# One encoder layer on one core: a third of the feed-forward block products in a seven-product form, weight sums on VectorE, the feed-forward axis in four chunks

## The chip, the core and the metric

The kernel runs on one core of a Trainium2 chip. The time is device microseconds (us) of one execution; the figure for the kernel before is the median of three runs. In the text PE is the matmul engine (TensorE), PEld its weight loads, DVE is VectorE, ACT is ScalarE, POOL is GpSimd, SP is SyncE, which issues most DMAs. PSUM is the memory in which matmuls accumulate: eight banks of 128 x 512 float32.

## What is computed

One layer over 256 tokens with 2048 features (D) and a feed-forward width (d_ff) of 5632. The two feed-forward networks (FFNs), one ahead of the mixers and one behind, are

```python
def swiglu(h, w1, w3, w2):
    return (jax.nn.silu(h @ w1) * (h @ w3)) @ w2

x = x + 0.5 * swiglu(rmsnorm(x, g1), w1, w3, w2)     # FFN 1
h = rmsnorm(x, g)
# h @ w_in, differential attention y_a, latent attention y_b
x = x + (sigmoid(g_a) * (y_a @ W_a) + sigmoid(g_b) * (y_b @ W_b)) @ W_out
x = x + 0.5 * swiglu(rmsnorm(x, g2), w1', w3', w2')  # FFN 2
```

Everything is float32. w1 and w3 are 2048 x 5632, w2 is 5632 x 2048. The 256 tokens are two blocks t of 128.

## The kernel before

**Precision.** Each large product runs as three passes in a reduced float32 format (fp32r): an operand v is split into hi (v rounded to fp32r) and lo = v - hi, and hi*hi + hi*lo + lo*hi accumulate in one PSUM bank. Activations are stationary (transposed, blocks of 128 x 128), weights move, 512 columns at a time. So one block product of 128 rows of weight, 512 columns and one token block is three matmuls (L144, L145, L146).

**A weight tile.** `gemm` takes the weight in tiles of KT = 2 blocks of 128 rows. For each tile SP loads `raw` (512 KB, L135), ACT casts it to `wh` (L105), DVE subtracts `wl = raw - wh` (L106), both in `split`, and PE runs 12 matmuls. There are four `raw` buffers and three each of `wh` and `wl`; a load waits until the subtraction that last read its buffer is done.

**What sets the order.** Each engine runs its instructions in the order in which the code issues them. Work that is not a weight tile (transposes, activation splits, attention pieces) is put on a list with `later`; `gemm` issues one step of it behind each weight tile, and all that is left before tile `due`.

**An FFN.** `ffn` runs over 11 chunks of 512 columns of d_ff, the "up" groups: the product with w1 (names f_u, 96 matmuls), silu on ACT (L242), the product with w3 (f_v, 96 matmuls), their product on DVE (L246). Four transposes per token block (L158, into f_t) and a split put the result in SBUF as G (f_ga, f_gb, f_gc: 44 blocks of 128). Then come the "down" products (f_d): for each of four 512-column chunks of w2 all 44 blocks, 264 matmuls into two banks, and x = x + 0.5 * PSUM on DVE (L261). Two to four banks are in use at a time, so the next product never shares a bank with one that is still being read.

**Around the FFNs.** FFN 1's x goes to DRAM (`x_mid`) while the mixers run. In the mixers the names are c, da, dav, mq, mk, ga, ba, gb, bb and wo for the products with w_in, the latent projections, the branches and W_out. mq has six blocks of 384 columns per job, mk four of 512. FFN 2's first product runs as part of the output stage.

## Time and profile before

| | us |
|---|---|
| median of 3 runs (2444.17 to 2445.04) | 2444.77 |
| span of the profiled execution, first to last instruction | 2442.6 |
| PE busy | 2429.4 |
| DVE busy | 1324.6 |
| ACT busy | 1111.9 |
| FFN 1: first up matmul to first down matmul | 10.9 to 503.7 |
| FFN 1: end of the down products | about 747 |
| last down matmul of FFN 2 starts | 2437.7 |

How to read the lines that follow in the text. A group line gives the source line, the engine, the operation, the tile written and the tiles read (buffer and job numbers left out), shape and type, the count, then total busy time in us and the mean of one in ns, then the idle time of the engine just before them and what ended it. A wait line gives who waited for whom: total us, how many times, the longest. A window line gives a stretch of the span and each engine's busy time in it. A DMA line gives a transfer's size and the median time from issue to landing. Busy time of PE counts a pipelined matmul until its modelled end, so the distance between starts, not the duration, is what a matmul costs.

### The profile page before, as it was taken

What the parts mean: (1) busy time and instruction counts of PE and PEld (TensorE: products, weight loads), DVE (VectorE), ACT (ScalarE), POOL (GpSimd) and SP (SyncE); (2) the same over time, 40 slices, a digit from 0 to 9 for tenths busy, and PEclk for the clock granted to TensorE, in tenths of its full rate; (3) what the DMA queues carried; (4) which work ended last, traced back from release to release, by engine and by line L of the source; (5) the groups of instructions that cost most, each with busy time, mean ns of one, the idle gap of its engine ahead of it and who ended that gap; (6) DMA issues with size and microseconds to landing.
All of it is one profiled execution on the core that took longest, in us unless ns stands there. A gap on an engine that the chain in (4) does not pass through costs nothing.

```text
span 2442.6 us, 29136 instructions
## 1 busy us (share of the span) xinstructions
PE 2429.4 (99%) x11070; PEld 2013.9 (82%) x11070; DVE 1324.6 (54%) x1865; ACT 1111.9 (46%) x1378; POOL 96.0 (4%) x144
## 2 busy tenths in 40 slices
PE   8999999999999999999999999999999999999999
PEld 7888888888889888888888888888888888888887
DVE  5445445445555666666665665655545545444444
ACT  5444444434444555545545554444444444443333
...
PEclk9999999999999999999999999999999999999999
...
GB/s 222 186 190 191 188 190 189 190 190 199 199 200 202 186 164 171 179 168 164 150 158 151 156 157 183 189 223 184 188 190 190 189 190 189 188 191 190 202 205 153
DMA packets 235867, 450.92 MB, mean 185 GB/s; under 512 B 14612, under 2 KB 27600, under 8 KB 235600
## 3 DMA queue, kind: packets, MB, share of 16 engines
...
## 4 chain that ended last, share of the span: by engine, by line
PE 41%; issue 9%; POOL 2%; DVE 1%; DMA 0%; ACT 0%; POOLq 0%; ACTq 0%; DVEq 0%
PE f_u L146 3%; PE f_u L144 3%; PE f_u L145 3%; PE f_v L144 3%; PE f_v L145 3%; PE f_v L146 3%; PE f_d L146 3%; PE f_d L144 3%; PE f_d L145 3%; PE wo L146 1%; PE wo L144 1%; PE wo L145 1%; PE bb L146 1%; PE bb L144 1%; PE bb L145 1%
## 5 line engine op out<-in xcount | busy, mean ns | idle before, releaser
L106 DVE TENSOR_TENSOR f_v_l<-f_v_w,f_v_h 128x1024 fp32r<-128x1024 f32 x176 | 215.5, 1225 | 261.3 <-ACT f_v_h L105 261.3
L106 DVE TENSOR_TENSOR f_d_l<-f_d_w,f_d_h 128x1024 fp32r<-128x1024 f32 x176 | 215.7, 1225 | 243.3 <-ACT f_d_h L105 243.3
L106 DVE TENSOR_TENSOR f_u_l<-f_u_w,f_u_h 128x1024 fp32r<-128x1024 f32 x176 | 215.6, 1225 | 220.8 <-ACT f_u_h L105 220.8
L105 ACT CAST f_d_h<-f_d_w 128x1024 fp32r<-128x1024 f32 x176 | 185.6, 1055 | 289.2 <-PE f_d L146 276.0
L105 ACT CAST f_u_h<-f_u_w 128x1024 fp32r<-128x1024 f32 x176 | 185.3, 1053 | 282.5 <-PE f_u L146 175.6
L105 ACT CAST f_v_h<-f_v_w 128x1024 fp32r<-128x1024 f32 x176 | 185.1, 1053 | 239.6 <-PE f_v L146 168.3
L144 PE MATMUL f_u<-f_u_h,hT 128*128 128x512 f32 x704 | 278.4, 396 | 0.0
L145 PE MATMUL f_u<-f_u_l,hT 128*128 128x512 f32 x704 | 274.7, 390 | 0.5 <-DVE f_u_l L106 0.5
L146 PE MATMUL f_u<-f_u_h,hT 128*128 128x512 f32 x704 | 274.9, 391 | 0.0
L144 PE MATMUL f_v<-f_v_h,hT 128*128 128x512 f32 x704 | 273.9, 389 | 0.0
L145 PE MATMUL f_v<-f_v_l,hT 128*128 128x512 f32 x704 | 273.9, 389 | 0.0
L146 PE MATMUL f_v<-f_v_h,hT 128*128 128x512 f32 x704 | 273.9, 389 | 0.0
L146 PEld LDWEIGHTS f_u<-f_u_h,hT 128*128 128x128 f32 x704 | 132.3, 188 | 28.0
L145 PEld LDWEIGHTS f_u<-f_u_l,hT 128*128 128x128 f32 x704 | 132.6, 188 | 27.2 <-DVE f_u_l L106 0.7
L146 PEld LDWEIGHTS f_v<-f_v_h,hT 128*128 128x128 f32 x704 | 132.2, 188 | 27.5
L144 PEld LDWEIGHTS f_v<-f_v_h,hT 128*128 128x128 f32 x704 | 132.2, 188 | 27.4
L145 PEld LDWEIGHTS f_v<-f_v_l,hT 128*128 128x128 f32 x704 | 132.2, 188 | 27.4
L144 PEld LDWEIGHTS f_u<-f_u_h,hT 128*128 128x128 f32 x704 | 132.3, 188 | 26.1
L144 PE MATMUL da<-da_h,hTm 128*128 128x512 f32 x256 | 103.9, 406 | 0.0
L144 PE MATMUL f_d<-f_d_h,f_ga 128*128 128x512 f32 x256 | 100.5, 393 | 0.0
L146 PE MATMUL da<-da_h,hTm 128*128 128x512 f32 x256 | 100.2, 391 | 0.0
L106 DVE TENSOR_TENSOR da_l<-da_w,da_h 128x1024 fp32r<-128x1024 f32 x64 | 78.2, 1223 | 40.5 <-ACT da_h L105 40.1
(313 smaller groups left out, 4765.2 us busy)
## 6 DMA issues: line engine op xcount, KB each, us to landing
f_u_w<-in_ffn_w SPq DMA_DIRECT2D x176, 512.0 KB, 3.8
f_v_w<-in_ffn_w SPq DMA_DIRECT2D x176, 512.0 KB, 3.7
f_d_w<-in_ffn_w SPq DMA_DIRECT2D x176, 512.0 KB, 4.3
da_w<-in_w_in SPq DMA_DIRECT2D x64, 512.0 KB, 3.8
dav_w<-in_w_in SPq DMA_DIRECT2D x32, 512.0 KB, 3.8
ga_w<-in_w_in SPq DMA_DIRECT2D x32, 512.0 KB, 3.7
ba_w<-in_w_branch_a SPq DMA_DIRECT2D x32, 512.0 KB, 4.1
gb_w<-in_w_in SPq DMA_DIRECT2D x32, 512.0 KB, 4.3
```

What stands on the lines that cost most here:

```text
L105: nc.scalar.copy(out=hi, in_=src)
L106: nc.vector.tensor_sub(out=lo, in0=src, in1=hi.bitcast(F32))
L144: nc.tensor.matmul(out=o, lhsT=hi(kb, t), rhs=wh[:, j], start=first, stop=False)
L145: nc.tensor.matmul(out=o, lhsT=hi(kb, t), rhs=wl[:, j], start=False, stop=False)
L146: nc.tensor.matmul(out=o, lhsT=lo(kb, t), rhs=wh[:, j], start=False, stop=last)
```

## The change

**Seven products for eight.** Take two blocks of 128 rows (k), two token blocks and two blocks of 512 columns: a 2 x 2 by 2 x 2 block product. The plain form has eight block products of three matmuls, 24 matmuls. Strassen's form (as arranged by Winograd) has seven, 21 matmuls, with sums of blocks on both sides ahead of them and sums of the results behind them. `gemm2` goes through a product in such pairs of k blocks; a table says which pair is plain ("P") and which in the seven-product form ("S"): three of the eight pairs of each up group (TKINDS), 7 of the 22 pairs of G (GKINDS, cyclic over the 11 groups). In an up group the two column blocks are the chunk of w1 (`left`) and of w3 (`right`), so both products run together; in a down product they are two neighbouring 512-column blocks of w2.

**Weight tiles.** A tile now holds four blocks: of a pair 2 k blocks by 2 column blocks, 1 MB, loaded by two DMAs of 512 KB. For an S pair DVE makes three sums (L318, L319, L320; one overwrites a quarter of `raw`), then `raw` (2048 columns) and the sums (1536) are split. There are two buffers each of `raw`, `wh`, `wl`, and a third during the FFNs only (pool `w7`). In the mixers `gemm` fills the same tiles in halves of two blocks.

**Accumulators.** All seven are used, one PSUM bank each (q1 to q7), the eighth bank is for transposes. P pairs add into q5, q2, q3, q4. Behind the last S pair q1 is copied (ACT, L336) and q6, q7 are added (DVE, L337, L338); behind the last pair q5, q2, q3, q4 (L346 to L355), all into one tile `ev`. The next block's first matmuls wait until DVE has read the bank.

**Activations.** `put_pairs` stores, for each pair, 7 (S) or 6 (P) blocks: DVE makes the sums (L281 to L284, L287), then a split. The gain is applied on DVE (L274), G's factor 0.5 on ACT (L272).

**Four chunks.** The down products run behind up groups 2, 5, 8 and 10, over the blocks made since the last time (6, 6, 4 and 6 pairs), in two halves of 1024 columns. The first three chunks' results are added to x in DRAM (`x_mid`) by an accumulating DMA on GpSimd's queue, 1 MB each; the last chunk loads x back and adds it in its evictions. G then needs less SBUF, which the larger weight tiles take.

**Smaller moves.** `ptf`, `rot` and `gate` have one buffer for two; FFN 2's first product starts behind the output stage and not in it; x's stores go to GpSimd's queue.

```diff
-KT = 2
+KT = 4
...
-    wp = ctx.enter_context(tc.tile_pool(name="wp", bufs=3))
+    wp = ctx.enter_context(tc.tile_pool(name="wp", bufs=2))
+    def wtile(tag, dt, name):
+        i = turnover[tag] = (turnover.get(tag, -1) + 1) % (3 if "w7" in pools else 2)
+        if i < 2:
+            return wp.tile([P, KT, NW], dt, tag=f"{tag}{i}", bufs=1, name=name)
+        return pools["w7"].tile([P, KT, NW], dt, tag=tag, bufs=1, name=name)
...
-            raw = wp.tile([P, KT, n], F32, tag="raw", bufs=4, name=f"{name}_w")
-            wh = wp.tile([P, KT, n], F32R, tag="wh", name=f"{name}_h")
-            wl = wp.tile([P, KT, n], F32R, tag="wl", name=f"{name}_l")
+            if k0 % KT == 0:
+                full = [wtile("raw", F32, f"{name}_w"), wtile("wh", F32R, f"{name}_h"), wtile("wl", F32R, f"{name}_l")]
+            raw, wh, wl = (f[:, k0 % KT:k0 % KT + kt, :n] for f in full)
...
+    SEVEN = (("q1", 0, "s", 1), ("q6", 5, "s", 0), ("q7", 2, "w", 1), ("q5", 4, "w", 0),
+             ("q2", 1, "s", 2), ("q3", 6, "s", 3), ("q4", 3, "w", 2))
+    PLAIN = (("q5", 2, 0), ("q2", 0, 1), ("q3", 4, 0), ("q4", 2, 1))
...
+        def sums():
+            for a, (kind, T, _) in enumerate(pairs):
+                g = f[0][:, a]
+                if kind == "S":
+                    nc.vector.tensor_sub(out=g[:, 4], in0=g[:, 2], in1=g[:, 3])
+                    nc.vector.tensor_sub(out=g[:, 5], in0=g[:, 4], in1=g[:, 0])
+                    nc.vector.tensor_add(out=g[:, 6], in0=g[:, 1], in1=g[:, 5])
+                    nc.vector.tensor_sub(out=g[:, 2], in0=g[:, 0], in1=g[:, 2])
+                    n = 7
+                else:
+                    nc.vector.tensor_sub(out=g[:, 4:6], in0=g[:, 0:2], in1=g[:, 2:4])
+                    n = 6
+                split(T[:, 0], T[:, 1], g[:, :n])
+        return [partial(turn, t) for t in range(NT)] + [sums]
+    def gemm2(left, right, pairs, name, due=None, x=None):
+        q = {k: pools["acc"].tile([P, NW], F32, tag=k, bufs=1, name=f"{name}_{k}") for k in ("q1", "q2", "q3", "q4", "q5", "q6", "q7")}
+        ev = pools["ev"].tile([P, NT, 2 * NW], F32, tag="ev", bufs=1, name=f"{name}_e")
+        e11, e12, e21, e22 = ev[:, 0, 0:NW], ev[:, 0, NW:], ev[:, 1, 0:NW], ev[:, 1, NW:]
+        lastS = max(i for i, p in enumerate(pairs) if p[0] == "S")
+        n, started = len(pairs), set()
+        def three(o, T, slot, bh, bl, stop):
+            for x, b, end in ((T[:, 0, slot], bh, False), (T[:, 0, slot], bl, False), (T[:, 1, slot], bh, stop)):
+                nc.tensor.matmul(out=q[o], lhsT=x, rhs=b, start=o not in started, stop=end)
+                started.add(o)
+        for i in range(n):
+            if i == due:
+                flush()
+            kind, T, k = pairs[i]
+            raw = wtile("raw", F32, f"{name}_w")
+            nc.sync.dma_start(out=raw[:, 0::3], in_=right(k))
+            nc.sync.dma_start(out=raw[:, 1:3], in_=left(k))
+            h4 = lambda m: (wtile("wh", F32R, f"{name}_h{m}"), wtile("wl", F32R, f"{name}_l{m}"))
+            if kind == "S":
+                sm = pools["w7"].tile([P, 3, NW], F32, tag="sum", bufs=1, name=f"{name}_s")
+                nc.vector.tensor_tensor(out=sm[:, 0:2], in0=raw[:, 0:1].to_broadcast([P, 2, NW]), in1=raw[:, 1::2], op=ALU.add)
+                nc.vector.tensor_add(out=raw[:, 0], in0=sm[:, 0], in1=raw[:, 3])
+                nc.vector.tensor_add(out=sm[:, 2], in0=raw[:, 0], in1=raw[:, 2])
+                sh, sl = h4("s")
+                split(sh, sl, raw)
+                wh, wl = h4("w")
+                split(wh[:, 0:3], wl[:, 0:3], sm)
+                B = {"s": (sh, sl), "w": (wh, wl)}
+                for o, slot, b, u in SEVEN:
+                    three(o, T, slot, B[b][0][:, u], B[b][1][:, u], o in ("q1", "q6", "q7") and i == lastS)
+            else:
+                ph, pl = h4("p")
+                split(ph, pl, raw)
+                for o, slot, right_side in [(o, s, 1 - l) for o, s, l in PLAIN]:
+                    for j in range(2):
+                        u = 3 * j if right_side else 1 + j
+                        three(o, T, slot + j, ph[:, u], pl[:, u], i == n - 1 and j == 1)
+            if i == lastS:
+                nc.scalar.copy(out=e11, in_=q["q1"])
+                nc.vector.tensor_add(out=e12, in0=q["q6"], in1=e11)
+                nc.vector.tensor_add(out=e21, in0=q["q7"], in1=e12)
+                if x is not None:
+                    (x11, x12), (x21, x22) = ((x[:, t, 0:NW], x[:, t, NW:]) for t in range(NT))
+                    nc.vector.tensor_add(out=x11, in0=x11, in1=e11)
+                    nc.vector.tensor_add(out=x21, in0=x21, in1=e21)
+                    nc.vector.tensor_sub(out=x22, in0=x22, in1=e21)
+            if pend:
+                pend.pop(0)()
+        nc.vector.tensor_sub(out=e12, in0=q["q5"], in1=e12)
+        if x is None:
+            nc.vector.tensor_sub(out=e22, in0=q["q5"], in1=e21)
+            x11, x12, x21 = e11, e12, e21
+        else:
+            nc.vector.tensor_add(out=x22, in0=q["q5"], in1=x22)
+            nc.vector.tensor_add(out=x12, in0=x12, in1=e12)
+        nc.vector.tensor_add(out=x11, in0=q["q2"], in1=x11)
+        nc.vector.tensor_add(out=x12, in0=q["q3"], in1=x12)
+        nc.vector.tensor_add(out=x21, in0=q["q4"], in1=x21)
+        return ev
+    TKINDS, GKINDS = "PSPPSPSP", ("PS", "PP", "SP")
+    GROUPS = DFF // NW
+    DOWN = {2: (0, 1, 2), 5: (3, 4, 5), 8: (6, 7), 10: (8, 9, 10)}
...
+        G = {}
+        for g in range(GROUPS):
+            ev = gemm2(rows(w1, g * NW), rows(w3, g * NW), T, f"{name}_u{g}", due=5 if g == 0 else None)
+            for t in range(NT):
+                r = rstd[:, t:t + 1]
+                nc.scalar.activation(out=ev[:, t, 0:NW], in_=ev[:, t, 0:NW], func=AF.Silu, scale=r)
+                nc.vector.scalar_tensor_tensor(out=ev[:, t, 0:NW], in0=ev[:, t, NW:], scalar=r, in1=ev[:, t, 0:NW],
+                                               op0=ALU.mult, op1=ALU.mult)
+            G[g] = [(k, v, 4 * g + 2 * i) for i, (k, v) in enumerate(places[2 * (g % 3):2 * (g % 3) + 2])]
+            later(*put_pairs(G[g], lambda t, ev=ev: ev[:, t, 0:NW], None, f"{name}{g}"))
+            if g not in DOWN:
+                continue
+            last = g == GROUPS - 1
+            if last:
+                xl.append(big.tile([P, NT, D], F32, tag=tagX, name=f"{name}_x"))
+                pend[0:0] = [partial(load_x, t, 0) for t in range(NT)]
+                later(*(partial(load_x, t, 1) for t in range(NT)))
+            pairs = [p for i in DOWN[g] for p in G[i]]
+            for n in range(2):
+                ns = slice(n * 2 * NW, (n + 1) * 2 * NW)
+                ev = gemm2(rows(w2, n * 2 * NW), rows(w2, n * 2 * NW + NW), pairs, f"{name}_d{g}{n}",
+                           due=len(pairs) - 2 if n == 0 else None, x=xl[0][:, :, ns] if last else None)
+                if last:
+                    for t, h in ((1, 1), (0, 0), (0, 1), (1, 0)):
+                        done(xl[0], t, 2 * n + h)
+                else:
+                    nc.gpsimd.dma_start(out=xdram[:, :, ns], in_=ev, accum_op=ALU.add)
...
-                nc.vector.scalar_tensor_tensor(out=x[:, t, cs], in0=po[t], scalar=0.5, in1=x[:, t, cs],
-                                               op0=ALU.mult, op1=ALU.add)
...
+        nc.gpsimd.dma_start(out=xdram[:, t, cs], in_=x[:, t, cs])
+        later(partial(chunk_done, x, t, c, Tm[0], "mix_norm_g", f"m{c}{t}"))
...
+            nc.gpsimd.dma_start(out=xdram[:, :, cs], in_=x[:, :, cs])
+            later(*ffn_put(x, T, c, "ffn2_norm_g", f"o{c}"))
-        first = gemm(a["ffn2_w1"][0][:, 0:NW], NW, allk, *operand(T), "f2_u0", due=4)
```

The first place: VectorE where one up group ends and the next begins, in FFN 1. f1_u4 is group 4's product with w1, f1_v3 group 3's with w3; `_w`, `_h`, `_l` are `raw`, `wh`, `wl`. Before:

```order
L106 TENSOR_TENSOR f1_v3_l_1424<-f1_v3_w_1421,f1_v3_h_1423 128x1024 [waits DMAHW1_49,Activation_49]
L106 TENSOR_TENSOR f1_u4_l_1446<-f1_u4_w_1443,f1_u4_h_1445 128x1024 [waits DMAHW2_49,Activation_49]
L106 TENSOR_TENSOR f1_u4_l_1464<-f1_u4_w_1461,f1_u4_h_1463 128x1024 [waits DMAHW3_49,Activation_49]
L246 SCALAR_TENSOR_TENSOR f1_s30_1289<-f1_v3_0_1293,rstd_n1_90,f1_s30_1289 128x512 [waits PE_49]
L246 SCALAR_TENSOR_TENSOR f1_s31_1291<-f1_v3_1_1294,rstd_n1_90,f1_s31_1291 128x512 [waits PE_49]
L106 TENSOR_TENSOR f1_u4_l_1489<-f1_u4_w_1486,f1_u4_h_1488 128x1024 [waits DMAHW4_49,Activation_49]
```

And of the change (`_e` is the tile `ev`, `_s` the weight sums, `_lp`, `_ls`, `_lw` the low parts of a plain tile, of an S pair's `raw` and of its sums):

```order
L318 TENSOR_TENSOR f1_u4_s_1897<-f1_u4_w_1894 128x1024 [waits DMAHW5_49,DMAHW4_49,DVE_49]
L338 TENSOR_TENSOR f1_u3_e_1572<-f1_u3_q7_1571,f1_u3_e_1572 128x512 [waits DVE_49,PE_49]
L121 TENSOR_TENSOR f1_u4_lp_1860<-f1_u4_w_1856,f1_u4_hp_1859 128x2048 [waits DMAHW3_49,DMAHW2_49,Activation_49]
L346 TENSOR_TENSOR f1_u3_e_1572<-f1_u3_q5_1569,f1_u3_e_1572 128x512 [waits DVE_49,PE_49]
L348 TENSOR_TENSOR f1_u3_e_1572<-f1_u3_q5_1569,f1_u3_e_1572 128x512
L353 TENSOR_TENSOR f1_u3_e_1572<-f1_u3_q2_1566,f1_u3_e_1572 128x512 [waits PE_49]
L354 TENSOR_TENSOR f1_u3_e_1572<-f1_u3_q3_1567,f1_u3_e_1572 128x512 [waits DVE_49,PE_49]
L355 TENSOR_TENSOR f1_u3_e_1572<-f1_u3_q4_1568,f1_u3_e_1572 128x512 [waits DVE_49,PE_49]
L395 SCALAR_TENSOR_TENSOR f1_u3_e_1572<-f1_u3_e_1572,rstd_n1_97 128x512 [waits DVE_49,Activation_49]
L319 TENSOR_TENSOR f1_u4_w_1894<-f1_u4_s_1897,f1_u4_w_1894 128x512
L395 SCALAR_TENSOR_TENSOR f1_u3_e_1572<-f1_u3_e_1572,rstd_n1_97 128x512 [waits Activation_49]
L320 TENSOR_TENSOR f1_u4_s_1897<-f1_u4_w_1894 128x512 [waits DVE_49]
```

Where two operations stood between weight subtractions there are now the eviction of seven banks and the sums of an S pair, and L318, which waits for its tile's load, stands ahead of all evictions but L337.

The second place: PE at the same seam. Before, the first rows of group 4's product follow the last of group 3's and wait for the cast alone (the subtraction is waited for by the second row):

```order
L145 MATMUL f1_v3_1_1294<-f1_v3_l_1424,hT1_89 128x512
L146 MATMUL f1_v3_1_1294<-f1_v3_h_1423,hT1_89 128x512
L144 MATMUL f1_u4_0_1441<-f1_u4_h_1445,hT1_89 128x512 [waits Activation_49]
L145 MATMUL f1_u4_0_1441<-f1_u4_l_1446,hT1_89 128x512 [waits DVE_49]
L146 MATMUL f1_u4_0_1441<-f1_u4_h_1445,hT1_89 128x512
```

After, each bank's first matmul also waits for DVE's eviction of that bank (x2: two in a row):

```order
L305 MATMUL f1_u3_q4_1568<-f1_u3_hp_1811,hT1p_96 128x512
L305 MATMUL f1_u4_q5_1852<-f1_u4_hp_1859,hT1p_96 128x512 [waits DVE_49,Activation_49]
L305 MATMUL f1_u4_q5_1852<-f1_u4_lp_1860,hT1p_96 128x512
L305 MATMUL f1_u4_q5_1852<-f1_u4_hp_1859,hT1p_96 128x512 x2
L305 MATMUL f1_u4_q5_1852<-f1_u4_lp_1860,hT1p_96 128x512
L305 MATMUL f1_u4_q5_1852<-f1_u4_hp_1859,hT1p_96 128x512
L305 MATMUL f1_u4_q2_1849<-f1_u4_hp_1859,hT1p_96 128x512 [waits DVE_49]
```

The group's product now begins in q5, which was the fourth bank from the end of the group before, and each later bank brings a wait of its own.

The third place: SP at the start of FFN 2. wo3 is the last W_out product; the tile numbers tell the three buffers apart:

```order
L152 DMA wo3_w_12943<-in_w_out 128x2x512 [waits DMAHW5_49,DMAHW4_49,DVE_49]
L152 DMA wo3_w_12943<-in_w_out 128x2x512
L313 DMA f2_u0_w_13005<-in_ffn2_w3 128x2x512 [waits DMAHW7_49,DMAHW6_49,DVE_49]
L314 DMA f2_u0_w_13005<-in_ffn2_w1 128x2x512
L313 DMA f2_u0_w_13076<-in_ffn2_w3 128x2x512 [waits DMAHW1_49,DMAHW0_49,DVE_49]
L314 DMA f2_u0_w_13076<-in_ffn2_w1 128x2x512
L313 DMA f2_u0_w_13038<-in_ffn2_w3 128x2x512 [waits DVE_49,PE_49,Pool_49]
L314 DMA f2_u0_w_13038<-in_ffn2_w1 128x2x512
```

The load of 13038, the second pair's tile in the third buffer, waits for PE and POOL besides DVE, and every load behind it on SP waits with it; before, SP's rows here wait only for a subtraction on DVE.

More of the change, by code (lines that the diff above doesn't have):

```diff
@@ new lines, in pair_views, with put_pairs, turn @@
+    def pair_views(t, n, w):
+        return [t[:, i * 2 * w:(i + 1) * 2 * w, :].rearrange("p (h s) k -> p h s k", h=2) for i in range(n)]
+    def put_pairs(pairs, srcs, gain, name):
+        f = []
+        def turn(t):
+            if t == 0:
+                f.append(pools["pt"].tile([P, 2, 7, P], F32, tag="pf", bufs=1, name=f"pf_{name}"))
+            src = srcs(t)
+            tp = transposes(lambda i: src[:, i * P:(i + 1) * P], 4, f"tp_{name}{t}")
+            o, i_ = f[0][:, :, 2 * t:2 * t + 2], tp.rearrange("p (a b) k -> p a b k", a=2)
+            if gain is None:
+                nc.scalar.activation(out=o, in_=i_, func=AF.Copy, scale=0.5)
+            else:
+                nc.vector.tensor_tensor(out=o, in0=i_, in1=gain.rearrange("p (a b) -> p a b", a=2).unsqueeze(3)
+                                        .to_broadcast([P, 2, 2, P]), op=ALU.mult)
+        def sums():
[12 more added lines that the diff above has]
+        return [partial(turn, t) for t in range(NT)] + [sums]
@@ new lines, in tile_block, with with_kinds, ffn_T @@
+    TKINDS, GKINDS = "PSPPSPSP", ("PS", "PP", "SP")
+    GROUPS = DFF // NW
+    DOWN = {2: (0, 1, 2), 5: (3, 4, 5), 8: (6, 7), 10: (8, 9, 10)}
+    def with_kinds(kinds, tS, tP):
+        tS, tP = list(tS), list(tP)
+        return [(k, (tS if k == "S" else tP).pop(0)) for k in kinds]
+    def ffn_T(tagS, tagP, name):
+        nS = TKINDS.count("S")
+        nP = len(TKINDS) - nS
+        tS = pair_views(big.tile([P, nS * 14, P], F32R, tag=tagS, name=f"{name}s"), nS, 7)
+        tP = pair_views(big.tile([P, nP * 12, P], F32R, tag=tagP, name=f"{name}p"), nP, 6)
+        return [(k, v, 2 * i) for i, (k, v) in enumerate(with_kinds(TKINDS, tS, tP))]
@@ new lines, in tile_block, with fetch @@
+    xdram = nc.dram_tensor("x_mid", (P, NT, D), F32, kind="Internal").ap()
+    f1 = ExitStack()
+    enter(f1, "w7", bufs=1)
+    enter(f1, "ev", bufs=1)
+    enter(f1, "acc", bufs=1, space=bass.MemoryType.PSUM)
+    pool = pools["pt"] = f1.enter_context(tc.tile_pool(name="f1", bufs=1))
+    x = big.tile([P, NT, D], F32, tag="D", name="x1")
+    T = ffn_T("C", "A", "hT1")
+    def fetch(c):
+        for t in range(NT):
+            cs = slice(c * NW, (c + 1) * NW)
+            nc.sync.dma_start(out=x[:, t, cs], in_=xin[:, t, cs])
@@ new lines, in put, with sums @@
+    def put(c):
+        return ffn_put(x, T, c, "ffn1_norm_g", f"i{c}")
+    rstd, step = rms_of_x("n1")
+    def sums():
+        for c in range(D // NW):
+            for t in range(NT):
+                chunk_sum(x, t, c, f"i{c}{t}")
+        step()
+        nc.gpsimd.dma_start(out=xdram, in_=x)
+    fetch(0)
+    gain_columns(0)
+    for s in put(0):
+        s()
+    run = lambda *ss: (lambda: [s() for s in ss])
+    later(run(partial(fetch, 1), *put(1)), run(partial(fetch, 2), partial(fetch, 3)), run(*put(2)), run(*put(3)), sums,
+          partial(gain_columns, 1))
@@ L315, in tile_block @@
+    ptx = ExitStack()
+    enter(ptx, "pt", bufs=1)
+    rstd, step = rms_of_x("n2")
+    later(step)
+    w_in = a["w_in"][0]
+    hi, lo = operand(Tm[0])
+    c_job = lambda j: gemm(w_in[:, O_C + j * 448:O_C + (j + 1) * 448], 448, allk, hi, lo, f"c{j}", due=4)
+    first = c_job(0)
+    ptx.close()
     ctx_merge = ExitStack()
```

158 lines of the change are left out of this document (62 added, 96 removed).

## Prediction

> **What bounds the kernel now.** I read the first two parts of the page, then the windows, then the list of waits.
>
> ```profile
> span 2442.6 us, 29136 instructions
> PE 2429.4 (99%) x11070; PEld 2013.9 (82%) x11070; DVE 1324.6 (54%) x1865; ACT 1111.9 (46%) x1378; POOL 96.0 (4%) x144
> PE   8999999999999999999999999999999999999999
> DVE  5445445445555666666665665655545545444444
> PEclk9999999999999999999999999999999999999999
> ```
>
> PE is busy in every slice at the full clock, and DVE has about half of its time left. The windows show two up groups (a 512-column chunk of w1 and of w3 with the transposes of one chunk) and a stretch of the down products; columns are us, busy time of PE, PEld, DVE, ACT, POOL with counts, PEclk, DMA share, GB/s:
>
> ```profile
> 120.00:164.50 44.50, 44.50 (x202) 36.82 (x201) 22.13 (x21) 19.09 (x20) 0.00 (x0) 1.00 0.64 189
> 164.50:209.00 44.50, 44.50 (x202) 36.82 (x201) 22.14 (x21) 19.09 (x20) 0.00 (x0) 1.00 0.65 190
> 520.00:564.00 44.00, 44.00 (x196) 36.44 (x195) 20.09 (x17) 16.88 (x16) 0.00 (x0) 1.00 0.62 196
> ```
>
> PE never pauses: one group takes 44.50 us. The waits point the same way:
>
> ```profile
> ACT f_d_h L105 <- PE f_d L146: 276.0, 167, 1.7
> DVE f_d_l L106 <- ACT f_d_h L105: 243.3, 170, 1.5
> ACT f_u_h L105 <- PE f_u L146: 175.6, 106, 1.7
> ```
>
> ACT waits for PE to free a buffer and DVE waits for ACT; nobody feeds PE late. So the end is set by the count of matmuls times their pitch:
>
> ```profile
> 305.57 0.39 PE L145 MATMUL f_v<-f_v_l,hT 128*128 128x512 f32 x1
> 308.29 0.39 PE L145 MATMUL f_v<-f_v_l,hT 128*128 128x512 f32 x1
> ```
>
> The second row is twelve matmuls behind the first: 2.72/12 = 0.2267 us each (0.39 is one with its pipeline). An up group's 192 make 43.5 us; 1.0 us is left for eight transposes.
>
> **What the change removes.** A P pair keeps 24 matmuls; an S pair has 21. Per FFN the up part has 11 x 3 S pairs and the down part 7 x 2: 47 x 3 = 141 matmuls fewer, 282 in both. If PE stays saturated this is 282 x 0.2267 = 63.9 us. An up group becomes 183 x 0.2267 + 1.0 = 42.5 us. The order of instructions has 9318 matmuls of 512 columns against 9600, so "the change doesn't do what it says" gets no chance.
>
> **What it adds on DVE.** Nearest rows:
>
> ```profile
> L106 DVE TENSOR_TENSOR f_u_l<-f_u_w,f_u_h 128x1024 fp32r<-128x1024 f32 x176 | 215.6, 1225 | 220.8 <-ACT f_u_h L105 220.8
> L106 DVE TENSOR_TENSOR mq_l<-mq_w,mq_h 128x768 fp32r<-128x768 f32 x24 | 23.0, 958 | 27.1 <-ACT mq_h L105 27.1
> L106 DVE TENSOR_TENSOR c_l<-c_w,c_h 128x896 fp32r<-128x896 f32 x24 | 26.2, 1092 | 22.7 <-ACT c_h L105 22.7
> L106 DVE TENSOR_TENSOR f_ga<-f_t,f_ga 128x512 fp32r<-128x512 f32 x16 | 10.9, 684 | 0.0
> L569 DVE TENSOR_TENSOR kh<-kr,r_mk 128x128 f32<-128x128 f32 x16 | 4.2, 305 | 0.0
> L246 DVE SCALAR_TENSOR_TENSOR f_s<-f_v,rstd_n,f_s 128x512 f32<-128x512 f32 x44 | 30.9, 744 | 0.0
> L105 ACT CAST f_u_h<-f_u_w 128x1024 fp32r<-128x1024 f32 x176 | 185.3, 1053 | 282.5 <-PE f_u L146 175.6
> L105 ACT CAST mq_h<-mq_w 128x768 fp32r<-128x768 f32 x24 | 20.0, 835 | 25.1 <-issue 16.2 <-ACT me L585 3.6 <-PE dav L146 3.5
> ```
>
> From 768 to 1024 elements a subtraction grows by 267 ns, 1.04 ns an element. So by extension 1536 elements cost 1.76 us and 2048 cost 2.29; an ACT cast grows by 0.85 ns, and 2048 cost 1.93. These two sizes stand in no row; the line through 512, 768, 896 and 1024 is straight within 0.02 us, and I see no room for more than 0.1 either way.
>
> A P pair costs DVE 2.29 us beside 24 x 0.2267 = 5.44 on PE. An S pair costs 1.23 + 0.69 + 0.69 (the three sums) + 2.29 + 1.76 = 6.66 beside 4.76: **DVE is slower than PE in each S pair and regains it in the P pairs.** For one up group: 3 x 6.66 + 5 x 2.29 = 31.4; seven evictions at 0.684 = 4.8; two L395 at 0.744 = 1.5; the sums and splits of the transposed result, 2.25 for an S pair (four of 0.29, one of 1.09) and 1.38 for a P pair (0.42, 0.96), by the 7 S and 15 P pairs of 11 groups 3.3. Together 41.0 us against PE's 42.5.
>
> To that come DVE's own waits. In an S pair the cast of the raw tile (1.93) can start only after L319 and must end before the subtraction; DVE has only L320 (0.69) to do meanwhile, as the order shows: about 1.3 us, three times, 3.9. Against it stands an overlap:
>
> ```profile
> 332.47 1.23 DVE L106 TENSOR_TENSOR f_u_l<-f_u_w,f_u_h 128x1024 fp32r<-128x1024 f32 x1 [1.49 <-ACT f_u_h L105]
> 333.61 0.68 DVE L106 TENSOR_TENSOR f_gb<-f_t,f_gb 128x512 fp32r<-128x512 f32 x1
> 746.49 1.37 DVE L261 SCALAR_TENSOR_TENSOR x<-f_d,x 128x512 f32<-128x512 f32 x2
> ```
>
> The second instruction starts 1.14 us after the first, which lasts 1.23: 0.09 saved where the next operation waits for nothing. About 20 of a group's 35 operations are so placed (L319, L320, L338, L354 and others wait for a DVE result): 1.7 saved. DVE then needs 41.0 + 3.9 - 1.7 = 43.2, just over PE's 42.5, and some waits are filled by an eviction. I take **43.1 per up group: 11 x (43.1 - 44.5) = -15.4 per FFN.**
>
> [...]
>
> **The down products.** Before: 4 x 264 x 0.2267 = 239.4 us per FFN. PE's least afterwards is (14 x 21 + 30 x 24) x 0.2267 = 229.9. But the products are now eight short blocks (three chunks of 6 pairs, one of 4, two halves each), with one bank per accumulator: a block's first matmuls wait for the evictions of the one before. I went through the rows of PE, ACT and DVE in their order with the durations above. That gives 65.0 for the two halves of each of the first two chunks (PE's least 62.6), 43.2 for the four-pair chunk (42.2), 68.8 for the last, which begins with an S pair and has ten evictions: 242.0, **+2.6**. So an FFN's loops take 729 - 12.8 (before: 11 x 44.5 + 239.4).
>
> **Loads.**
>
> ```profile
> f_u_w<-in_ffn_w SPq DMA_DIRECT2D x176, 512.0 KB, 3.8
> x<-x_mid SPq DMA_DIRECT2D x1, 2048.0 KB, 9.8
> x_mid<-x SPq DMA_DIRECT2D x8, 256.0 KB, 5.1
> ```
>
> A pair is now two loads of 512 KB on SP, issued together. 189 GB/s at a share of 0.64 is 295 GB/s at full use, so the second adds 1.8: 5.6 us. The line to 2 MB gives 5.8, nothing gained by going together 7.6. This matters at one place: the raw tile of a group's last S pair is freed only by its subtraction, its successor's load waits for that in SP's queue, and the next group's first L318 waits for the load at the head of DVE's queue, with the evictions L338 to L355 queued behind it that PE needs. With a landing of 5.4 the same walk gives 714.5 per FFN, with 5.8 719.8, with 6.5 734, with 7.2 755: beyond about 5.5 the wait is no longer covered. At 5.6 it is 717, the -12.8 above within a microsecond.
>
> GpSimd adds twelve accumulating stores of 1 MB. No row shows one. At 295 GB/s it reads and writes for some 7 us beside weight loads; the DMA share of 0.64 leaves room for this. From 0 to 25 (each delays one load by 1 MB / 295 GB/s = 3.6, of which some 1.5 is covered); I take **+4**, nearer to hidden. L336 on ACT also waits for the store before, in the four-pair chunk some 10 us behind its issue: a store that lands later stops ACT's casts there once per FFN; that is inside the 25.
>
> **The seams.** In FFN1's first group DVE makes the activation sums, 19 us where before it had 11: first group **+2** (0 to 8). FFN1's end has the ten evictions and the next stage's transposes on one DVE queue: **+3** (0 to 6). The mixers now have two weight tiles of four blocks in place of four of two:
>
> ```profile
> 700.00:1100.00 400.00, 400.00 (x1874) 337.32 (x1874) 246.92 (x507) 200.85 (x302) 30.47 (x32) 1.00 0.61 179
> ```
>
> PE has no gap there, so any stall counts. A 512-column tile is 5.4 us of PE work and covers a load and split (3.8 + 2.3), but an mq job's six blocks leave a half-filled tile: 6.1 us of cover against 6.1. Eight such jobs at 0 to 1 us: **+3**. In FFN2's first group the second pair's load waits on SP for the output projection's last matmul, as the third buffers lie in that stage's memory; every later load is queued behind it. 5.6 us to land and then an S pair's sums and casts, against the one pair that PE has in hand: **+3** (0 to 6). The tail is the same.
>
> **Sum.** -12.8 + 2 + 3 (FFN1), +3 (mixers), -12.8 + 3 (FFN2), +4 (stores) = -10.6: span 2442.6 - 10.6 = 2432.0. The median of the runs, 2444.77, is 2.2 above the profiled span; with that, **2434 us**. Its own range, by the ends of the seams and stores and landings of 5.4 to 6.0, is 2415 to 2455.
>
> **The rivals.**
> 1. *DVE's starts do not overlap.* For: the row at 746.49, and many new operations read the result just made. Against: 1.14 us at 332.47. A group is then 41.0 + 3.9 = 44.9, less a little filling, some 44.7; the walk gives 739 to 744 per FFN. 24 more each: **2482**, slower. It decides as soon as DVE needs over 44.5 per group.
> 2. *Loads land late.* For: two loads share the engines, and the stores join them; x_mid's 256 KB already take 5.1. Against: a DMA share of 0.64. At 6.5 +17 per FFN: **2468**, slower; at 7.2 2508. Break-even against before lies at about 6.0.
> 3. *PE stays saturated.* DVE's waits are filled by other rows and the loads come at 5.4 or earlier: 2442.6 - 63.9 + 2.2 = **2381**, a few us more with the seams. For: 41.0 is below 42.5. Against: 6.66 against 4.76 in each S pair.
>
> **How the numbers follow.** Forecast's own range 0.50, rival 1 0.15, rival 2 0.19, rival 3 0.16. Within 0.2% (about what a measurement of this kernel can tell from no change) means 2440 to 2450: of the forecast's 0.50 some 0.11 lie there and 0.04 above; of rivals 1 and 2 0.02 each in it. Faster 0.35 + 0.16 = 0.51, same 0.15, slower 0.34. The range 2398 to 2485 leaves out half of rival 3 and the worse half of rival 2, some 0.2.
>
> **What would show it.** Windows of an up group: 43.1, and DVE busy about 41 in it. DVE's total near 1930 us (94 times three sums 244, longer splits 123, evictions 105 up and 74 down, activation sums 59). PE's share falls to about 97%, its idle time in front of the first S pair of groups and at block starts, ended by DVE. Rival 1 shows as DVE without a gap and groups over 44.5; rival 2 as L318 waiting for a DMA, landings over 6; rival 3 as PE at 99%. Wrong altogether it would be if a stage outside the FFNs moved by more than 8 us.

## The result: 0.7% slower

The changed kernel takes 2461.89 us (median of four runs, 2460.68 to 2463.17) against 2444.62 us: a ratio of 1.0072, 95% interval 1.0058 to 1.0086. Run once more beside the later experiments (e14 below) it took 2457.55, ratio 1.0049 [1.0034, 1.0064]. The forecast was 2434, faster. The time lies inside the range on record (2398 to 2485), on the wrong side of no change. (Brackets behind a ratio are its 95% interval; each ratio is to the kernel before, measured beside that run.) Two executions, one of e2 (8419 us, mean granted clock 0.28, the one that its trace shows, at full clock through FFN 1 alone) and one of e8 (2641 us, 0.853), ran at a lower granted clock and are left out of the medians.

The first parts of the page of the kernel after, its weight loads and its stores (KB each, median us to landing):

```profile
span 2459.6 us, 28650 instructions
PE 2401.8 (98%) x10788; PEld 1956.4 (80%) x10788; DVE 1866.9 (76%) x2363; ACT 1241.1 (50%) x1290; POOL 133.8 (5%) x177
DVE  7987887888896666756665664556888898788798
...
f_u_w<-in_ffn_w SPq DMA_DIRECT2D x352, 512.0 KB, 4.7
f_d_w<-in_ffn_w SPq DMA_DIRECT2D x176, 512.0 KB, 5.0
x_mid<-f_d_e POOLq DMA_DIRECT2D x12, 1024.0 KB, 9.4
```

The 282 matmuls are gone (11070 to 10788), but PE's busy time fell by only 27.6 us, not by 63.9 (the window of an up group below reads as fully busy, 43.7 us of 43.7, although its 183 matmuls at the 0.2267 us of before make 41.5 and its transposes, by before's windows, 1.0), and PE is idle for 57.8 us of the span where it was for 13.2. In the FFNs (the first and last quarter of the slices) DVE now stands at 7 to 9 tenths. In the names of blocks u4 is up group 4, d20 and d21 are the two halves of the chunk behind group 2, and so on to d100 and d101; a block's length is counted from its first matmul to the next block's. Windows of the kernel after: one around u4, then two second halves (d21 of FFN 1, d51 of FFN 2), each with the store of its first half beside it:

```profile
262.80:306.50 43.70, 43.70 (x195) 35.28 (x193) 39.56 (x39) 23.93 (x18) 0.00 (x0) 1.00 0.59 193
186.20:219.80 33.60, 32.12 (x140) 25.59 (x138) 26.18 (x22) 14.73 (x9) 1.22 (x1) 1.00 0.73 220
2087.70:2124.50 36.80, 33.62 (x139) 26.66 (x138) 26.50 (x22) 14.71 (x9) 1.08 (x1) 0.95 0.70 201
```

The up group itself takes 43.0 (the window is 0.7 wider), close to the forecast's 43.1. A second half needs 31.3 us of matmuls and took 33.6 and 36.8, though DVE is busy for only 26 of them. The waits say for whom PE and DVE stood:

```profile
DVE f_u_s L318 <- DMA f_u_w<-in_ffn_w: 24.9, 10, 4.2
DVE f_d_s L318 <- DMA f_d_w<-in_ffn_w: 20.5, 11, 5.1
PE f_d_q L305 <- DVE f_d_lp L121: 15.4, 11, 2.8
PE f_u_q L305 <- DVE f_u_lp L121: 13.8, 14, 2.1
```

L318, the first sum of an S pair, waited 45 us for weight loads, and PE waited 29 us for the low parts of *plain* pairs. One such place, DVE in the second half d51 of FFN 1:

```profile
391.40 2.28 DVE L121 TENSOR_TENSOR f_d_lp<-f_d_w,f_d_hp 128x2048 fp32r<-128x2048 f32 x1
398.14 1.23 DVE L318 TENSOR_TENSOR f_d_s<-f_d_w 128x1024 f32<-128x1024 f32 x1 [4.46 <-DMA f_d_w<-in_ffn_w]
399.29 2.29 DVE L121 TENSOR_TENSOR f_d_lp<-f_d_w,f_d_hp 128x2048 fp32r<-128x2048 f32 x1
```

ACT's cast for that second subtraction, and PE at the same place:

```profile
393.10 1.91 ACT L120 CAST f_d_hp<-f_d_w 128x2048 fp32r<-128x2048 f32 x1 [2.14 <-PE f_d_q L305]
```

```profile
401.63 0.50 PE L305 MATMUL f_d_q<-f_d_lp,f_gp 128*128 128x512 f32 x1 [2.22 <-DVE f_d_lp L121]
```

The subtraction at 399.29 belongs to a plain pair whose cast had ended at 395.0 (393.10 + 1.91). It stood behind an L318 whose load had not landed, and PE stood behind it.

### The profile page after: what moved, and what is told of

The parts are those of the page before. It is cut to its first block, busy times and chain, and to the rows that moved or that the text cites. A ratio compares the mean times of both kernels' runs of the same rounds, so it can differ in the third digit from the quotient of the medians.

```text
span 2459.6 us, 28650 instructions
## 1 busy us (share of the span) xinstructions
PE 2401.8 (98%) x10788; PEld 1956.4 (80%) x10788; DVE 1866.9 (76%) x2363; ACT 1241.1 (50%) x1290; POOL 133.8 (5%) x177
## 3 DMA queue, kind: packets, MB, share of 16 engines
q0 software_dynamic: 6064, 23.10, 4.1%
## 4 chain that ended last, share of the span: by engine, by line
PE 25%; issue 23%; POOL 2%; DVE 2%; ACT 1%; DMA 1%; POOLq 0%; SPq 0%; DVEq 0%; ACTq 0%
PE f_u_q L305 3%; PE f_d_q L305 2%; PE ms L557 1%; PE wo L161 1%; PE wo L159 1%; PE wo L160 1%; PE bb L160 1%; PE bb L159 1%; PE bb L161 1%; PE gb L160 1%; PE gb L159 1%; PE gb L161 1%; PE ba L159 1%; PE ba L160 1%; PE ba L161 1%
## 5 line engine op out<-in xcount | busy, mean ns | idle before, releaser
L305 PE MATMUL f_d_q<-f_d_hp,f_gp 128*128 128x512 f32 x960 | 306.7, 395 | 1.6 <-DVE f_u_e L348 1.5
L120 ACT CAST f_u_hp<-f_u_w 128x2048 fp32r<-128x2048 f32 x110 | 210.4, 1912 | 148.3 <-PE f_u_q L305 90.9
L305 PE MATMUL f_u_q<-f_u_hp,hT1p 128*128 128x512 f32 x880 | 283.5, 395 | 0.8 <-ACT f_u_hp L120 0.6
L305 PE MATMUL f_u_q<-f_u_hp,hT2p 128*128 128x512 f32 x880 | 279.9, 391 | 1.5 <-DVE f_u_e L348 0.9
L121 DVE TENSOR_TENSOR f_u_lp<-f_u_w,f_u_hp 128x2048 fp32r<-128x2048 f32 x110 | 251.5, 2286 | 38.5 <-ACT f_u_hp L120 38.5
L305 PEld LDWEIGHTS f_d_q<-f_d_hp,f_gp 128*128 128x128 f32 x960 | 182.3, 190 | 41.7 <-issue 4.0
L305 PE MATMUL f_d_q<-f_d_lp,f_gp 128*128 128x512 f32 x480 | 190.6, 397 | 15.5 <-DVE f_d_lp L121 15.4
L305 PEld LDWEIGHTS f_u_q<-f_u_hp,hT1p 128*128 128x128 f32 x880 | 167.1, 190 | 38.4 <-issue 2.9
L305 PE MATMUL f_u_q<-f_u_lp,hT1p 128*128 128x512 f32 x440 | 174.2, 396 | 7.3 <-DVE f_u_lp L121 7.3
L305 PE MATMUL f_u_q<-f_u_lp,hT2p 128*128 128x512 f32 x440 | 172.5, 392 | 6.6 <-DVE f_u_lp L121 6.5
```

The source lines that it names most:

```text
L120: nc.scalar.copy(out=hi, in_=src)
L121: nc.vector.tensor_sub(out=lo, in0=src, in1=hi.bitcast(F32))
L305: nc.tensor.matmul(out=q[o], lhsT=x, rhs=b, start=o not in started, stop=end)
```

## Where the 17 us lie

From the starts of the first c and wo matmuls the span falls into three stages. (In the tile's row: count, min/median/max ns, first and last start.) Before, then after:

```profile
L144 PE MATMUL c<-c_h,hTm x96: 362/365/452, 747.0 to 805.6; 128*128 128x448 f32 x96
L144 PE MATMUL wo<-wo_h,mT x128: 387/389/477, 1617.2 to 1707.5; 128*128 128x512 f32 x128
```

```profile
L159 PE MATMUL c<-c_h,hTm x96: 360/368/471, 750.8 to 813.8; 128*128 128x448 f32 x96
L159 PE MATMUL wo<-wo_h,mT x128: 387/389/477, 1629.7 to 1720.0; 128*128 128x512 f32 x128
```

FFN 1 became 3.8 us longer (747.0 to 750.8), the mixers 8.7 (870.2 to 878.9), the output product and FFN 2 4.5 (825.4 to 829.9). So both FFNs lost all of their gain and the mixers became slower.

## Experiments

Four theories were open: **stores** (the accumulating stores make loads late, and L318 at the head of DVE's queue hands that to PE), **DVE work** (the S pairs' sums and evictions are simply too much), **structure** (chunks, seams and evictions cost the time whatever the pairs are), and **tiles** (the mixers' four-block buffers).

### e1: no stores

```diff
-                else:
-                    nc.gpsimd.dma_start(out=xdram[:, :, ns], in_=ev, accum_op=ALU.add)
```

> The twelve accumulating stores of 1 MB are left out (the first three chunks' down results are dropped), all else as in the changed kernel (2461.9 us). Theory 'stores': a store's traffic makes the weight loads beside it land late, L318 waits for one at the head of DVE's queue, and PE stalls 2 to 5 us in the second half of each chunk and in the group behind it. Then these stalls (some 14 us per FFN) go: 2434 to 2442 us, L318's waits for a DMA fall from 45 us to under 10. Rival 'DVE work': the blocks without an up group behind them are bound by DVE's evictions and sums; then the stalls stay: 2457 to 2462 us. (The store's own reading of ev, for which L336 waited 4.5 us in all, goes in both.)

Measured: 2424.16 us, ratio 0.9917 [0.9903, 0.9932]. The stores cost 38 us (33 against e14's 2457.55), more than the theory said, and without them the change is 0.8% faster than the kernel before. An up group and the two second halves of above, now without stores:

```profile
257.50:300.50 43.00, 43.00 (x192) 34.90 (x191) 38.87 (x37) 23.93 (x18) 0.00 (x0) 1.00 0.59 196
184.00:215.90 31.90, 31.77 (x139) 25.66 (x138) 26.19 (x22) 14.72 (x9) 0.00 (x0) 1.00 0.61 199
2061.70:2094.00 32.30, 31.78 (x140) 25.69 (x138) 26.60 (x22) 14.72 (x9) 0.00 (x0) 1.00 0.60 197
```

The second halves fall from 33.6 and 36.8 to 31.9 and 32.3 with the same DVE work (26.2 and 26.6 us), so DVE's work is not what bound them. By the starts of the blocks' first matmuls, the twelve blocks that run right behind a store (the second halves and the up groups after them) give 33 us of the two FFNs' 37. Another 2.8 us lie in FFN 1's first group, ahead of any store: its length differs between executions that have the same order there (51.2 to 54.7).

### e2 and e6: all pairs plain, with and without stores

```diff
-    TKINDS, GKINDS = "PSPPSPSP", ("PS", "PP", "SP")
+    TKINDS, GKINDS = "PPPPPPPP", ("PP", "PP", "PP")
```

(with evictions that leave out q1, q6 and q7; e6 also leaves out the stores, as e1 does)

> All pairs plain (9600 matmuls again, no weight sums), the pairs, chunks, stores and weight tiles of the change kept. It prices the restructuring alone. If the new structure itself costs nothing in the FFNs, an up group takes 44.5 us, a half chunk of six pairs 32.6 and of four 21.8, and with the mixers' +9 the time is 2452 to 2458 us. Theory 'stores': loads are late here too, but no L318 stands at DVE's head, a plain pair's load has DVE slack of 3 us behind it: at most 5 us more, 2455 to 2462. Rival 'structure': block seams and stores stall PE whatever the pairs are: the second halves stay 2 to 4 us over their matmuls and the time is over 2466.

> All pairs plain and the twelve stores left out (the first three chunks' down results are dropped). With e1 (2424), e2 (2478) and the changed kernel (2462) it closes a table of two by two: S pairs or not, stores or not. If the stores hurt only where L318 stands in line, they cost little here: 2470 to 2478. If they delay PE through any load, they cost some 20 to 38 us here too: 2440 to 2458, and then what is left over the kernel before is the mixers' 5 and the seams.

| us | with stores | without |
|---|---|---|
| a third in seven products | 2461.89 | 2424.16 |
| all plain | 2478.44 | 2478.82 |

The ratios of the lower row to the kernel before are 1.0136 [1.0119, 1.0153] and 1.0139 [1.0124, 1.0154]. With plain pairs the same stores cost nothing: DVE has slack (57% busy in e6, whose line follows) and no L318 stands in its queue. In FFN 1 the second half d21 takes 32.64 us in both, which is its 144 matmuls and nothing more.

```profile
PE 2441.9 (99%) x11070; PEld 2019.8 (82%) x11070; DVE 1408.7 (57%) x1805; ACT 1086.5 (44%) x1158; POOL 112.0 (5%) x165
```

So neither part has this cost alone: it takes the store and the S pair together. The restructuring alone costs 34 us, where e2's first expectation had 8 to 14. That is over the 2466 of the rival 'structure', but not by its mechanism: the second halves take no more than their matmuls. (e6 lies just over the 2470 to 2478 expected where stores hurt only beside L318.) By stages e6 is 12.7 us longer than before in FFN 1, 6.6 in the mixers and 15.7 in the output product and FFN 2. Most of what the FFNs lose lies at two places. One is the last chunk's first half (d100), 41.9 us for 32.6 of matmuls in both FFNs, where PE waits 5.1 us each time for G's casts and the clock then drops (3.4 us lost each time):

```profile
L305 PE MATMUL f_d_q<-f_d_hp,f_gp 128*128 128x512 f32 x1216 | 386.8, 395 | 10.1 <-ACT f_gp L120 10.1
```

The other is FFN 2's first group, 51.1 us where the kernel before has 44.5; PE waits 4.5 us for a cast there. In e1 these blocks take 33.4 and 45.1. So the column without stores does not show what the seven products alone are worth: of its 54.7 us some 18 are stalls at these places that only the all-plain form has. An up group falls from 44.5 to 42.8, 1.7 of the 2.0 us that nine matmuls take. Why the plain form stalls at these two places stays open.

### e7: stores that do not add

```diff
-                    nc.gpsimd.dma_start(out=xdram[:, :, ns], in_=ev, accum_op=ALU.add)
+                    nc.gpsimd.dma_start(out=xdram[:, :, ns], in_=ev)
```

> The twelve stores write without adding (x_mid then holds the last chunk's partial sums; same bytes written, nothing read back). Theory 'bytes': the cost follows the DMA time that the store takes from the loads; without the read it is some 3.5 us at full use in place of 5 to 6, so about half of the 38 us goes: 2438 to 2450. Rival 'issue' (GpSimd's queue itself, or the wait of the next eviction for the store's end, costs the time): 2457 to 2463.

Measured: 2427.45 us, 0.9935 [0.9919, 0.9952]: 34 of the 38 us are gone, more than the half that was expected. GpSimd's DMA queue (packets, MB, share of 16 engines' span), in the kernel after and in e7:

```profile
q0 software_dynamic: 6064, 23.10, 4.1%
```

```profile
q0 software_dynamic: 6064, 23.10, 2.5%
```

The same 23.10 MB take 100.8 us of all 16 engines with the addition and 60.6 without. Less the 28 us that this queue has in e1, which has no stores, one store takes 6.1 us with the addition and 2.7 without. A window around one store of the kernel after shows what that does to the loads beside it; a window without a store, in the group before, and one around the same store in e7 stand behind it:

```profile
f_d_w<-in_ffn_w SPq DMA_DIRECT2D x5, 512.0 KB, 6.4
x_mid<-f_d_e POOLq DMA_DIRECT2D x1, 1024.0 KB, 10.7
```

```profile
f_d_w<-in_ffn_w SPq DMA_DIRECT2D x8, 512.0 KB, 4.5
```

```profile
f_d_w<-in_ffn_w SPq DMA_DIRECT2D x3, 512.0 KB, 4.7
x_mid<-f_d_e POOLq DMA_DIRECT2D x1, 1024.0 KB, 7.6
```

Over all twelve stores the FFNs' weight loads that are in flight beside one take 6.4 us (median of 62) in the kernel after and 4.8 (of 34) in e7; the others take 4.7 and 4.5.

The next eviction's own wait for the store's end occurs twice in the kernel after, in the second half of the four-pair chunk (d81) of each FFN:

```profile
ACT f_d_e L336 <- DMA x_mid<-f_d_e: 4.5, 2, 2.2
```

It is a second path to PE. ACT's copy L336 waits for the store, DVE's L337 for the copy, and a plain pair's low part, queued behind L337, is late for PE (FFN 1):

```profile
581.00 0.59 ACT L336 COPY f_d_e<-f_d_q 128x512 f32<-128x512 f32 x1 [2.24 <-DMA x_mid<-f_d_e]
581.62 0.69 DVE L337 TENSOR_TENSOR f_d_e<-f_d_q,f_d_e 128x512 f32<-128x512 f32 x1 [2.05 <-ACT f_d_e L336]
584.57 0.50 PE L305 MATMUL f_d_q<-f_d_lp,f_gp 128*128 128x512 f32 x1 [2.24 <-DVE f_d_lp L121]
```

A drop of the clock follows in both FFNs (PEclk 0.66 in the window from 585 to 590 us, 0.67 from 2290 to 2295). d81 takes 25.6 us in both, and 21.9 in e1 and e7, so some 7 of the 37 us lie here. So the cost is not the issue on GpSimd (e7 has it too) but the DMA time of the addition: it makes late the loads beside it, which is the larger part, and the store itself, for which L336 waits.

### e4 and e5: L318 later in DVE's queue

e4 queues each L318 behind the low part of the pair ahead; e5 does so only in the blocks that run right behind a store:

```diff
+    LATE = ("d21", "d51", "d81", "u3", "u6", "u9")
...
-                nc.vector.tensor_tensor(out=sm[:, 0:2], in0=raw[:, 0:1].to_broadcast([P, 2, NW]), in1=raw[:, 1::2], op=ALU.add)
+                with (tc.issue_after(wlow[0]) if name[3:] in LATE else nullcontext()):
+                    nc.vector.tensor_tensor(out=sm[:, 0:2], in0=raw[:, 0:1].to_broadcast([P, 2, NW]), in1=raw[:, 1::2], op=ALU.add)
```

(`wlow[0]` is the last low part issued ahead; `issue_after` puts L318 behind it in DVE's order.)

> The first weight sum (L318) of an S pair is queued on DVE behind the low part of the pair ahead of it; the same instructions otherwise. Theory 'head of queue': most of the stalls in the second halves and behind them (2 to 3 us each, six per FFN) come from a ready subtraction that stands behind an L318 whose load has not landed: 2440 to 2450 us, L318's waits for DMAs under 25 us. Rival 'DVE work' (or the load itself is what PE waits for): the S pair's own matmuls then wait in place of the plain pair's: 2457 to 2466.

> L318 queued behind the low part of the pair ahead, as in e4, but only in the six blocks per FFN that run right behind a store (d21, d51, d81, u3, u6, u9). e4's trace showed those blocks 12 us per FFN shorter than in the changed kernel and the others longer. Theory 'stores meet the head of DVE's queue': the six blocks keep e4's lengths, the others the changed kernel's: 2440 to 2448 us, and no clock dips behind these stalls. Rival 'DVE work': what is taken away here turns up in the next block: 2456 to 2464.

e4 took 2475.57 us, ratio 1.0121 [1.0104, 1.0138], slower than either expectation. The blocks behind stores did get shorter (d21 of FFN 1: 33.6 to 32.0), but elsewhere the S pair itself is now late, most of all in the first halves of the third and fourth chunk (d80 of FFN 1 27.6 us for 22.1, d100 44.7 for 33.3): ACT waited 351 us for L323 (the kernel after: 247 us for the same sum, L319).

```profile
ACT f_u_hs L120 <- DVE f_u_w L323: 245.0, 61, 7.6
ACT f_d_hs L120 <- DVE f_d_w L323: 105.8, 24, 7.3
```

e5 has the kernel after's instructions and stores; only twelve blocks have another order on DVE. It took **2430.67 us, ratio 0.9947 [0.9932, 0.9962]**: 31 us less than the changed kernel (27 less than e14), faster than the kernel before and below the 2440 to 2448 that were expected. L318 (now L324) waits 8 us for loads in place of 45, and PE 8 us for the low parts of plain pairs in place of 29:

```profile
DVE f_d_s L324 <- DMA f_d_w<-in_ffn_w: 4.2, 7, 0.9
DVE f_u_s L324 <- DMA f_u_w<-in_ffn_w: 3.6, 7, 0.9
PE f_d_q L310 <- DVE f_d_lp L121: 4.8, 4, 2.1
PE f_u_q L310 <- DVE f_u_lp L121: 2.9, 3, 1.8
```

and at the place shown above the low part no longer stands behind it:

```profile
388.26 2.29 DVE L121 TENSOR_TENSOR f_d_lp<-f_d_w,f_d_hp 128x2048 fp32r<-128x2048 f32 x1 [0.28 <-ACT f_d_hp L120]
391.47 1.23 DVE L324 TENSOR_TENSOR f_d_s<-f_d_w 128x1024 f32<-128x1024 f32 x1 [0.92 <-DMA f_d_w<-in_ffn_w]
```

d21 and d51 take 32.0 us in both FFNs, and the twelve blocks together 25 us less than in the changed kernel. So this place in the queue is where most of the stores' cost arises. What e5 leaves is mostly L336's wait, which it does not touch: d81 still takes 23.9 us in place of 21.9.

### e8: a fourth raw buffer in the FFNs

```diff
-        i = turnover[tag] = (turnover.get(tag, -1) + 1) % (3 if "w7" in pools else 2)
+        i = turnover[tag] = (turnover.get(tag, -1) + 1) % ((4 if tag == "raw" else 3) if "w7" in pools else 2)
```

> A fourth raw buffer in the FFNs (its 8 KB per partition found by letting ptf share pf's place). Loads can start a pair earlier. Theory 'late loads': L318's waits for DMAs (45 us) fall under 15 and the time to 2425 to 2442. Rival 'bandwidth': the store takes DMA time that must be made up later whatever the buffers are, with loads at a share of 0.6 that is small; then over 2455 only if DVE, not the load, is what is late.

Measured: 2441.33 us, 0.9984 [0.9974, 0.9993]; L318's waits for loads fell to 13.4 us. The late load was the lever here too. Yet it is 11 us slower than e5. Its last chunk's first half takes 40.8 us in both FFNs, e5's 33.2 and 33.1; PE waits there for ACT (3.6 us each), once more at the start of FFN 2 (4.9), and the clock drops behind these stalls (see the end): windows of 5 us sum to 17.1 us lost in e8 and none in e5. These are the places of e13 below.

### e3: the weight tiles alone, in the kernel before

```diff
-            raw = wp.tile([P, KT, n], F32, tag="raw", bufs=4, name=f"{name}_w")
+            if k0 % KT == 0:
+                full = [wp.tile([P, KT, NW], F32, tag="raw", name=f"{name}_w"),
...
+            raw, wh, wl = (f[:, k0 % KT:k0 % KT + kt, :n] for f in full)
```

(KT = 4, two buffers of each; ptf, rot and gate single; the scratch tile of the sums of squares, cst and rg as the change has them)

> The kernel before with only the change's weight tiles (four blocks each, two buffers, filled in halves) and its single ptf, rot and gate buffers; FFNs as before. Theory 'tiles': the mixers' loss of 8.7 us (c jobs 4.4, attention 3.6) comes from buffers that are freed only when four blocks are done: 2451 to 2457 us, the c jobs about 63 us from their first to their last matmul (58.6 before). Rival: the loss comes from the seams (pools reopened, evictions of FFN 1's last block beside c): then 2445 to 2447 and c stays at 58.6.

Measured: 2449.83 us, 1.0023 [1.0013, 1.0033]. From c's first matmul to wo's first:

```profile
L146 PE MATMUL c<-c_h,hTm x96: 362/365/452, 748.7 to 807.3; 128*128 128x448 f32 x96
L146 PE MATMUL wo<-wo_h,mT x128: 387/389/477, 1624.4 to 1714.6; 128*128 128x512 f32 x128
```

875.7 against 870.2: the tiles explain up to 5.5 of the 8.7 us, 1.7 of them a drop of the clock at 1133 us, which the kernel after does not have there. The c jobs are as before (58.6), so the c part of the expectation was wrong: that loss belongs to FFN 1's seam. The time is below the 2451 to 2457 of the theory and above the rival's 2447. e3 also lengthens FFN 1's first group by 2.2 us, with no activation sums in it.

### e11, e12, e13: towards a faster version

e11 is e5 with `raw`, `wh` and `wl` as two standing tiles each, so that a half of two blocks is freed by itself in the mixers. e12 adds the activation sums of FFN 1's first group on GpSimd, e13 adds e8's buffer to e11.

```diff
-            return wp.tile([P, KT, NW], dt, tag=f"{tag}{i}", bufs=1, name=name)
+            if (tag, i) not in kept:
+                kept[tag, i] = wp.tile([P, KT, NW], dt, tag=f"{tag}{i}", bufs=1, name=f"{tag}{i}")
+            return kept[tag, i]
```

> e5 (2430.7) and the weight tiles kept as two standing tiles, so that each half of two blocks is freed and loaded by itself in the mixers. Theory 'tiles': the mixers give back the 4 to 5 us that e3 showed in the mq and mk jobs: 2424 to 2428 us, FFNs as in e5. Rival: the mq jobs' loss comes from the single rot, ptf and gate buffers that e3 also had: 2430 to 2432.

> e11 with the activation sums of FFN 1's first group (20 operations of 128x128 and 128x256 on DVE, some 7 us) on GpSimd, which is idle there. Theory 'DVE work in the first group': u0 is bound by DVE (49 us busy of 54.7) and shortens by 3 to 6 us: 2419 to 2425. Rival: it is bound by the arrival of x and the chain transpose, gain, sums, split; GpSimd is slower at a sum and u0 grows: 2427 to 2435.

> e11 (2426.0) with e8's fourth raw buffer in the FFNs. If late loads still cost something behind the stores once L318 stands behind the low part, 2418 to 2424. Rival: e11's order already covers them, and the fourth buffer only lets more loads run beside the last chunk's reading of x, where e8 lost some 6 us per FFN: 2428 to 2440.

- e11: **2425.98 us, 0.9919 [0.9906, 0.9933]**, the fastest version that computes the whole layer, inside its 2424 to 2428. The mixers take 869.6 us, so the tiles' loss is gone.
- e12: 2428.84, 0.9933 [0.9921, 0.9946]: no gain, and inside the rival's 2427 to 2435. Three of the four 128x128 sums average 452 to 690 ns on GpSimd and the one that comes first 1019; on DVE they take 282 to 288. That the first group is bound by DVE's share of these sums is not borne out.
- e13: 2441.21, 0.9985 [0.9975, 0.9994], just over the rival's 2440. The first sum waits for loads for 1 us in all there, yet PE stalls for ACT at the last chunk (3.6 us in each FFN) and at the start of FFN 2 (4.9), and 17.0 us are lost to the clock. A fourth buffer does not pay in this form; why ACT is late there was not pursued.

### e14: the changed kernel again

> The changed kernel once more, beside the others on this chip: 2458 to 2466 us. If the dips of the granted clock follow the long stalls of PE, the trace shows 3 to 10 us lost to them again, behind stalls of 2 us and more; if they were chance, they lie elsewhere or are gone, and the time is 2455 or less.

Measured: 2457.55 us, just under the range. The stalls lie at the same places (44.5 us of L318's waits for loads). Three of the first trace's four drops of the clock come again (FFN 1's first group, d51 and d81 of FFN 2); one is gone and two are new (d21 of both FFNs).

## Why the prediction was wrong, by its steps

**The matmuls removed: right in number.** 282. Their worth of 63.9 us is not measured cleanly: e6 to e1 is 54.7, some 18 of it stalls of e6 (see there); in an up group it is 1.7 of 2.0 us.

**DVE in an up group: right in kind, a little high.** Predicted 41.0 us busy and 43.1 us a group; the windows show 38.9 to 39.6 busy. From the starts of the groups' first matmuls the mean of u1 to u10 is 42.8 without the stores and 43.5 with them. DVE's total was put at 1930 and is 1866.9. The overlap of starts, against which the first rival spoke, is there in these rows of the kernel after where nothing is waited for, and gone where the result just made is read:

```profile
376.83 0.68 DVE L337 TENSOR_TENSOR f_d_e<-f_d_q,f_d_e 128x512 f32<-128x512 f32 x1
377.62 0.69 DVE L338 TENSOR_TENSOR f_d_e<-f_d_q,f_d_e 128x512 f32<-128x512 f32 x1
...
379.55 0.69 DVE L346 TENSOR_TENSOR f_d_e<-f_d_q,f_d_e 128x512 f32<-128x512 f32 x1
380.15 0.68 DVE L348 TENSOR_TENSOR f_d_e<-f_d_q,f_d_e 128x512 f32<-128x512 f32 x1
```

L348 starts 0.60 us after L346 (0.69 long), 0.09 ahead of its end; L338, which reads L337's result, starts 0.79 after it (0.68 long), 0.11 behind its end.

**The down products: right without the stores.** Predicted 242.0 us per FFN; by block starts 240.2 (FFN 1) and 240.1 (FFN 2) in e1, but 248.4 and 251.0 in the changed kernel.

**The stores: the step that failed.** "I take **+4**, nearer to hidden", with 25 as the upper end; e1 measures 38 (33 against e14). The price of a store was not wrong: 7 us of all engines at full use, an estimate that counts a read and a write (no run shows the read itself), measured 6.1 (e7). What followed from it was. Each store was given one late load, by 3.6 us (half of that price, the bytes of a plain store) less 1.5 of cover; but 62 loads were in flight beside the twelve stores, and 30 of L318's 45 us of waits come with the stores (15 in e1). And the late load belongs to an S pair, whose L318 stands ahead of a plain pair's low part that is ready, so that PE stalls for work that had its data (e5: the order alone gives 25 us back in the blocks behind a store, with the stores in place). Behind some of these stalls the clock dropped as well (three in the kernel after, 1.7 us lost at each). L336's wait in the four-pair chunk was foreseen, once per FFN, and counted as inside the 25; it comes to some 7 us in both FFNs. The prediction named the wait (L318 at the head of DVE's queue) and put it at the up groups' seams, with ordinary loads; it is the loads beside a store that were late.

**The second rival** (late loads, 2468 us at a landing of 6.5) was the nearest, with the stores among its causes. Its mechanism is right beside a store alone: there the loads landed in 6.4 us, while the medians of all, 4.7 and 5.0, are below the 5.6 that the forecast itself used. That its total, worked out with every load at 6.5, lies 6 us from the measured one is in part luck.

**The seams.** FFN 1's end (+3) and the mq jobs (+3) show together in the mixers: +8.7 in this trace, +6.9 in e14's and +6.3 in e1's, against 6. The tiles give up to 5.5 of it (e3) and e11 undoes them. The sign "wrong altogether" (a stage outside the FFNs that moves by more than 8 us) is met in the first trace and not in e14's. FFN 1's first group was forecast at 48.5 us: 47.9 before, less 1.4 as in every group, and +2 (0 to 8). It takes 51.9 in e1 and 54.7 in the changed kernel, so that the term is 5.4 and 8.2: mis-sized. The cause given (DVE's sums) did not stand in e12; 2.2 us come with the weight tiles alone (e3). FFN 2's first group (+3, so 46.1 us) takes 45.4.

Without the stores the prediction's other terms sum to -14.6 us; e1's span is 21.5 below before's: up groups and down products came out a little better than forecast.
